# A half-swap of a 256 MB matrix by DMA alone: the sixteen engines on neighbouring rows instead of rows four apart

## The chip, the core and the metric

The kernel runs on one core of a Trainium2 chip. It uses none of the compute engines: all data is moved by the core's 16 DMA engines, straight from the input tensor in device memory (HBM) to the output tensor in the same memory. Two of the core's sequencers, SP (SyncE) and ACT (ScalarE), do nothing but issue DMA instructions and wait for older ones to land. Each of the two has a queue of its own, and both queues are served by the same 16 DMA engines.

The metric is the device time of one execution in microseconds (us). Beside it there is one profiled execution, whose trace records every DMA instruction, every DMA packet with its start and duration, and every semaphore wait.

## The reference

```
def setup_inputs():
    return {
        "x": np.random.randn(8192, 8192).astype(np.float32),
    }

def reference(x: np.ndarray) -> np.ndarray:
    return np.fft.ifftshift(x)
```

For an even number of rows and columns this shifts both axes by half: output row r is input row (r + 4096) mod 8192, and in each row the left and the right half change places. A row has 8192 float32 values, 32 KB; a half row, 16 KB, is the longest piece that stays in one piece. The matrix is 268.44 MB; all of it is read once and written once.

## The kernel before

The rows of the output are written in eight blocks of 1024 rows. Each block is written by eight DMAs, four on each queue. A DMA on SP's queue writes the left halves of 256 rows (reading the right halves of the source rows), and the DMA on ACT's queue that goes with it writes the right halves of the same rows (reading the left ones). So there are 32 DMAs on each queue, 64 in all, of 256 half rows, 4 MB, each.

Which 256 rows a DMA takes is in its access pattern, the list `dims` (line 30), which has three dimensions, each with a step in elements and a count:

- the outermost, `[STEP * C, ENGINES]`: 16 rows that lie STEP = 4 rows apart. This is the dimension over which a DMA is shared out to the 16 engines, one index for each.
- the middle one, `[STEP * ENGINES * C, per]`: each engine's own sequence of `per` = 16 rows, 64 rows apart.
- the innermost, `[1, hc]`: half a row, 4096 elements.

So at one moment the sixteen engines are to stand on sixteen rows that are 4 rows (128 KB) apart and cover 64 rows (2 MB), and each moves on by 64 rows. The loop on line 31 runs over the four rows `base` to `base + 3`: the first DMA of a block takes rows 0, 4, 8, ... of it, the next 1, 5, 9, ..., and after four the block is full. The pattern on the source side is the same, 4096 rows further on (modulo 8192).

There is no planner's order beyond this. The framework gives the DMAs eight semaphores in turn, so that each queue has four of its DMAs under way; before it issues the fifth, the sequencer waits until the first has landed. These waits carry the line of the DMA, L34; the waits at the end of the program carry L65, the line on which the tile context is left.

Of the kernel before, what the change touches and what calls it, by code (L numbers as in the profile page):

```python
# [1 line left out]

# [4 lines left out]


ENGINES = 16
STEP = 4  # L10


@with_exitstack
def kernel(
    ctx: ExitStack,
    tc: tile.TileContext,
    x: bass.AP,
    out: bass.AP,
):
    nc = tc.nc  # L20
    R, C = x.shape
    hr = R // 2
    hc = C // 2


    blocks = [(1024, 16)] * 8
    base = 0
    for rows, per in blocks:
        assert rows == STEP * ENGINES * per
        dims = [[STEP * C, ENGINES], [STEP * ENGINES * C, per], [1, hc]]  # L30
        for row in range(base, base + STEP):
            src_row = (row + hr) % R
            for eng, h in ((nc.sync, 0), (nc.scalar, hc)):
                eng.dma_start(  # L34
                    out=bass.AP(out.tensor, out.offset + row * C + h, dims),
                    in_=bass.AP(x.tensor, x.offset + src_row * C + hc - h, dims),
                )
        base += rows
    assert base == R


# [1 line left out]
_INS = ['x']  # L43
_OUTS = [((8192, 8192), 'float32')]


def kernel(**inputs):
    import numpy as _np
    import concourse.bacc as _bacc
    import concourse.tile as _tile  # L50
    from concourse import mybir as _mybir
    from concourse.bass_utils import run_bass_kernel_spmd as _run

    nc = _bacc.Bacc("TRN2", target_bir_lowering=False, num_devices=1)  # L54
    arrays, args = {}, []
    for name in _INS:
        a = _np.ascontiguousarray(inputs[name])
        if a.dtype.kind in "iu":
            a = a.astype(_np.int64)
        arrays[f"in_{name}_dram"] = a  # L60
        args.append(nc.dram_tensor(f"in_{name}_dram", a.shape, _mybir.dt.from_np(a.dtype), kind="ExternalInput").ap())
    for i, (shape, dtype) in enumerate(_OUTS):
        dt = _mybir.dt.from_np(_np.dtype(dtype))
        args.append(nc.dram_tensor(f"out_{i}_dram", shape, dt, kind="ExternalOutput").ap())
    with _tile.TileContext(nc) as tc:  # L65
        kernel(tc, *args)
    r = _run(nc, [arrays], core_ids=[0])
    got = tuple(r.results[0][f"out_{i}_dram"] for i in range(len(_OUTS)))
    return got[0]
```

## Time and profile before

| | |
|---|---|
| median of 3 runs | 824.26 us (824.24 to 824.76) |
| profiled execution, its span | 809.3 us |
| DMA instructions | 32 on SP, 32 on ACT, 4096 KB each |
| duration of a DMA instruction on its sequencer, median | 571 ns on SP, 578 ns on ACT |
| from issue to landing, shortest, median, longest | 25.1, 100.7, 103.1 us (both queues) |
| last DMA issued | at 705.9 us on SP, at 710.7 us on ACT |

The profiled execution's span runs from its first to its last recorded instruction; the device time of a run holds some work of the launch in addition. No other time than the span is known for the profiled execution.

A queue's share is the time that its packets took, as a part of what 16 engines have in the span. A packet here is one piece of up to 16 KB that one engine moves; packets under 512 bytes are the completions that an engine sends when its part of a DMA has landed. In a table of stretches the columns are: the stretch (us from the start of the span), its length, the busy time of the one compute engine that shows any work (GpSimd, four tiny instructions that set constants), the granted TensorE clock, the mean busy share of the 16 DMA engines (which can come out above 1 in short stretches, where a packet is counted whole), and the rate in GB/s, counted one way. In a list of waits the columns are who waited and on which line, for what, the total in us, the number of waits and the longest.

### The profile page before, as it was taken

Reading aid. Unit: us, or ns where it says so; the run is one execution under the profiler, and the core shown is the slowest. Engines: PE = TensorE matmul, PEld = TensorE weight load, DVE = VectorE, ACT = ScalarE, POOL = GpSimd, SP = SyncE. Lnnn points to the kernel's source line nnn. Section 1 sums busy time; section 2 is a strip of 40 time slices with the busy share of each in tenths; the row PEclk is TensorE's granted clock in tenths of the full one; section 3 lists DMA queues with packets and bytes.
Section 4 is the critical chain, followed back from the end, with each engine's and each line's share of the span. In section 5 each row is a group of like instructions: output and inputs, shape, how many; then the busy total and the mean of one; then the engine's idle time right before and its main releaser. Section 6 shows DMA issues by size and latency. Waiting matters only on the chain. (4 is left out here: it accounts for less than half of the span.)

```text
span 809.3 us, 109 instructions
## 1 busy us (share of the span) xinstructions
POOL 0.2 (0%) x4
## 2 busy tenths in 40 slices
POOL 0000000000000000000000000000000000000000
DMA  9999999999999999999999999999999999999998
GB/s 309 327 333 332 331 337 336 325 337 336 334 331 329 332 333 337 331 337 331 334 331 332 334 330 336 334 335 330 334 332 331 337 332 337 333 339 329 334 336 300
DMA packets 17408, 268.44 MB, mean 332 GB/s; under 512 B 1024, under 2 KB 1024, under 8 KB 1024
## 3 DMA queue, kind: packets, MB, share of 16 engines
q10 hardware_dynamic: 8704, 134.22, 49.9%
q1 hardware_dynamic: 8704, 134.22, 49.5%
HBM read 268.44 MB, written 268.44 MB: 663 GB/s over the span
## 5 line engine op out<-in xcount | busy, mean ns | idle before, releaser
L54 POOL MEMSET const-bfloat16-1.0<- 128x1 bf16 x1 | 0.1, 101 | 0.0
L54 POOL MEMSET const-uint8-127<- 128x1 uint8 x1 | 0.1, 101 | 0.0
L54 POOL MEMSET const-float32-0.0<- 128x1 f32 x1 | 0.1, 98 | 0.2 <-issue 0.2
L54 POOL MEMSET const-float32-1.0<- 128x1 f32 x1 | 0.1, 98 | 0.0
## 6 DMA issues: line engine op xcount, KB each, us to landing
out_dram<-in_x_dram ACTq DMA_DIRECT2D x32, 4096.0 KB, 100.7
out_dram<-in_x_dram SPq DMA_DIRECT2D x32, 4096.0 KB, 100.6
```

The lines of the kernel that those rows point to most:

```text
L54: nc = _bacc.Bacc("TRN2", target_bir_lowering=False, num_devices=1)
```

## The change

The constant STEP and the blocks go. A DMA now takes 512 neighbouring rows: its outermost dimension is 16 rows that lie one row (32 KB) apart, its middle one 32 steps of 16 rows (512 KB). There are 16 DMAs of 8 MB on each queue, 32 in all. The halves, the queues that they go to, and the order of the row ranges from the top down stay as they were.

```diff
-STEP = 4
...
-    blocks = [(1024, 16)] * 8
-    base = 0
-    for rows, per in blocks:
-        assert rows == STEP * ENGINES * per
-        dims = [[STEP * C, ENGINES], [STEP * ENGINES * C, per], [1, hc]]
-        for row in range(base, base + STEP):
-            src_row = (row + hr) % R
-            for eng, h in ((nc.sync, 0), (nc.scalar, hc)):
-                eng.dma_start(
-                    out=bass.AP(out.tensor, out.offset + row * C + h, dims),
-                    in_=bass.AP(x.tensor, x.offset + src_row * C + hc - h, dims),
-                )
-        base += rows
-    assert base == R
+    per = 32
+    dims = [[C, ENGINES], [ENGINES * C, per], [1, hc]]
+    for row in range(0, R, ENGINES * per):
+        src_row = (row + hr) % R
+        for queue, h in ((nc.sync, 0), (nc.scalar, hc)):
+            queue.dma_start(
+                out=bass.AP(out.tensor, out.offset + row * C + h, dims),
+                in_=bass.AP(x.tensor, x.offset + src_row * C + hc - h, dims),
+            )
```

## The prediction, made before the changed kernel was run

> **What bounds the kernel now.** I read the head of the page and its queue part first, because the kernel has no compute: the span, the number of packets, and how much of the sixteen DMA engines' time they fill.
>
> ```profile
> span 809.3 us, 109 instructions
> ...
> DMA packets 17408, 268.44 MB, mean 332 GB/s; under 512 B 1024, under 2 KB 1024, under 8 KB 1024
> ## 3 DMA queue, kind: packets, MB, share of 16 engines
> q10 hardware_dynamic: 8704, 134.22, 49.9%
> q1 hardware_dynamic: 8704, 134.22, 49.5%
> HBM read 268.44 MB, written 268.44 MB: 663 GB/s over the span
> ```
>
> The two queues fill 49.9 + 49.5 = 99.4% of the engines' time. Of 17408 packets, 1024 are tiny (64 DMAs with one completion on each of 16 engines), which leaves 16384 packets of 268.44 MB / 16384 = 16 KB: half a row each, 1024 per engine. One takes 0.994 x 809.3 us x 16 / 16384 = 0.786 us, and 1024 of them one after another make 804.6 us. So the end is set by what a 16 KB packet takes, and by nothing else.
>
> Second, stretches of the span, for what lies around the packets.
>
> ```profile
> core 0: us, POOL busy (x), PEclk, DMA share, GB/s
> 0.00:2.10 2.10, 0.20 (x4) 1.00 0.00 0
> 2.10:8.00 5.90, 0.00 (x0) 1.00 1.00 355
> 8.00:14.00 6.00, 0.00 (x0) 1.00 1.01 344
> ...
> 101.00:401.00 300.00, 0.00 (x0) 1.00 1.00 333
> ...
> 808.00:809.30 1.30, 0.00 (x0) 1.00 0.00 0
> ```
>
> Ahead of the first packet lie 2.1 us, behind the last 1.3: 3.4 us without data. The other 805.9 us move it at 333 GB/s, evenly from 100 us on, but faster (355, 344) in the first 12 us. The median of the runs, 824.26 us, is 15.0 us above the profiled span; I keep these 15.0 us unchanged, so a time is data + 3.4 + 15.0 = data + 18.4.
>
> Third, the waits of the issuing queue, to see whether a late DMA ever starves the engines.
>
> ```profile
> SPq L34 <- DMA out_dram<-in_x_dram: 686.6, 28, 25.0
> SPq L65 <- DMA out_dram<-in_x_dram: 101.9, 2, 79.4
> ...
> out_dram<-in_x_dram SPq DMA_DIRECT2D x32, 4096.0 KB, 100.6
> ```
>
> SP issues 32 DMAs and waits before 28 of them, at most 25.0 us; four are always under way, and one lands 100.6 us after its issue (four times 25.2 us). While it waits, three DMAs, some 75 us of work, lie ahead of the engines. Nothing is starved.
>
> Fourth, stretches cut by data: the span cut wherever another 1/512 of all bytes has moved, which is one row of 32 KB for every engine. Eight of them, from the middle:
>
> ```profile
> 510.81:512.28 1.47, 0.00 (x0) 1.00 1.10 368
> 512.28:513.96 1.68, 0.00 (x0) 1.00 0.84 283
> 513.96:515.48 1.52, 0.00 (x0) 1.00 1.10 356
> 515.48:517.16 1.68, 0.00 (x0) 1.00 0.94 312
> 517.16:518.64 1.48, 0.00 (x0) 1.00 1.10 365
> 518.64:520.24 1.60, 0.00 (x0) 1.00 0.93 317
> 520.24:521.77 1.53, 0.00 (x0) 1.00 1.10 353
> 521.77:523.46 1.69, 0.00 (x0) 1.00 0.91 301
> ```
>
> The second column is the time of one row step (the rate, in so short a stretch, depends on which packets' starts fall into it). Four steps take 1.47, 1.52, 1.48, 1.53, mean 1.50 us; the four between them 1.68, 1.68, 1.60, 1.69, mean 1.66. The work is the same, the engines are full in both; what differs is which rows the sixteen stand on and how they stand to each other. So a packet's price is not a constant of an engine, it depends by about 10% on the set of addresses under way at once. That is the quantity that this change touches. I also followed each engine through the trace (its next packet starts 3 to 4 ns before its last one ends): the sixteen alternate strictly between the queues, and their packet counts lie within 2 of each other at 50 us and within 6 at 600 us. They move almost in step, so "which addresses at once" is well described by the pattern.
>
> **The change, part by part.**
>
> *Bytes and packets.* The last dimension stays half a row, so there are again 16384 packets of 16 KB, 1024 an engine, one from the left and one from the right half in turn. Nothing is saved there: 0.
>
> *Half as many DMAs.* 32 instead of 64, 8 MB instead of 4. Each queue issues 16 fewer at 0.57 to 0.58 us (the issue rows' medians, 571 ns on SP and 578 on ACT): 9.2 us less on each of two queues that spend 686.6 us waiting. Hidden by the waits: 0. If four DMAs weren't queued ahead, the same 9.2 us would stand on the path; they are, and with 8 MB each, four of them cover about 200 us instead of 100. What is queued behind an issuing instruction is only the next issue.
>
> *Half as many completions.* 32 fewer tiny packets per engine. The rest of the data time beyond packets, 805.9 - 804.6 = 1.3 us, is all that 64 completions and the seams between DMAs can cost, so 32 of them cost 0 to 0.7 us. I take -0.3.
>
> *Start and end.* The first packet comes 1.4 us after the first issue at 0.73 us. An instruction with twice the rows could take up to twice that before its first packet: 0 to +1.4; the sixteen first packets start within 1 us of each other although each stands for 16 rows, so I take 0. At the end the last DMA of each queue is larger but an engine's share of the whole is not; the engines' packet counts differ by up to 6, which would cost up to 6 x 0.786 = 4.7 us if it all fell on the last engine, and the tail here costs about 1 us. -1 to +3.7, taken 0.
>
> *Where the engines stand.* Before, neighbouring engines were 4 rows (128 KB) apart, the sixteen covered 64 rows (2 MB), and the next step was 2 MB on; the rows between were filled by the next three DMAs. After, neighbours are 1 row (32 KB) apart, the sixteen read one closed piece of 512 KB and write one of 512 KB, and the next step is 512 KB on. The trace has no row for this distance. The bounds are the two kinds of row step: all 512 steps at 1.50 us make 768.0 us, time 786.4; all at 1.66 make 849.9, time 868.3. Today's mean, 805.9 / 512 = 1.574, is half of each. I take three slow to two fast: (3 x 1.66 + 2 x 1.50) / 5 = 1.596 us, x 512 = 817.2. Why on the slow side: today's fast steps alternate with slow ones, so whatever makes a step fast lasts for one step of 2 MB and depends on how the engines' addresses differ; the change makes them differ less, by a quarter of the distance both between engines and from step to step, and packs reads and writes alike into a quarter of the address range. With less difference between the addresses under way, I expect more of the unfavourable meetings than of the favourable ones. This is the weak term; the trace shows that placement matters, not which way.
>
> The Trainium skill ("DMA: Bandwidth & Descriptors", Latency and other measured facts) has a rule that speaks against my sign: copies between HBM tensors lost rate when rows lay a large power of two apart, 207 GB/s per direction at 512 KiB and 164 at 2 MiB. If it held for an engine's step, 2 MB before and 512 KB after, the data time would be 805.9 x 164 / 207 = 638 us and the time 657, an estimate from that page; if it held for the distance between neighbouring engines, both kernels would be on its good side and nothing would change. The row is 333 GB/s per direction at a step of 2 MB, above both of the page's figures, so I give the rule no weight in the sum.
>
> **Sum.** 817.2 (row steps) - 0.3 (completions) + 3.4 (around the data) = 820.3 us of span, + 15.0 = 835.3; I say 836 for the open ends of the start and the tail.
>
> **The rivals.**
>
> *The closed piece is served better (faster).* For it: placement is worth 10%, and the first 12 us, when all engines start level, run at 355 and 344 GB/s rather than 333; if neighbouring rows keep that opening rate (mean 350), 268.44 MB / 350 GB/s = 767 us, and half of that gain gives (805.9 + 767) / 2 = 786.5 us, time 804.9. Against it: the opening is also the time in which queues are still filling, and it lies at the old distance.
>
> *The rate belongs to the traffic, not to the place (no change).* For it: every long stretch gives 333 to 335 GB/s although the engines drift. Then only the small terms are left: 824.26 - 0.3 = 824.0, within 1% either way. Against it: the row steps above. The same time results if the change doesn't do what it says, because the engines drift: a few rows of drift are now as long as the distance between neighbours, and the pattern blurs.
>
> *All engines meet at one place (much slower).* Sixteen engines that stand at the same offset in neighbouring rows could get in each other's way at every step. Price: the longest of the row steps that I cut in this stretch, 529.52 to 531.31, 1.79 us; x 512 = 916 us, time 935. It decides as soon as the steps no longer alternate. Against it: at 4 rows' distance the opening steps show nothing of it.
>
> The Trainium skill ("HBM Reference", Specifications) gives about 716 GB/s for the memory of a pair of cores; 536.9 MB at that would be 750 us, time 768, an estimate, which would leave the faster rival room and no more; the row is 663 GB/s over the span.
>
> **How the numbers follow.** Moderately slower 0.45, much slower 0.08, faster 0.32, unchanged 0.15. What can be told from no change here is about 0.2%, 1.6 us; the unchanged case spreads by 1%, and gives 0.06 within that, 0.05 slower and 0.04 faster. So slower 0.45 + 0.08 + 0.05 = 0.58, faster 0.32 + 0.04 = 0.36, same 0.06. The likeliest case alone reaches from 826 to 868. The range goes from 786, all steps fast, to 878, all steps slow and 10 us for the way to the much slower case and the start and tail; some 0.06 lies below and 0.09 above.
>
> **What would show it.** Completions: 512 tiny packets instead of 1024. Depth: 100.6 us to landing should become about 204, with 12 waits on SP of about 51 us. The weak term: the packet, from the queues' shares, should rise from 0.786 to about 0.797 us, and more than half of the row steps should be long. If the packet falls, the sign is wrong, and the first rival holds; if it stays within 0.008 us, the second. If the queues' share falls well below 99%, the engines idle, and my statement that nothing starves is wrong.

## The result: 0.28% faster in the first comparison, and no change on another chip

The changed kernel took 821.94 us (median of 6 runs, 820.05 to 823.13), beside it the kernel before 824.38 us (823.05 to 824.86): a ratio of 0.9972, 95% interval 0.9962 to 0.9982. (A ratio here is worked out from all runs and can differ by up to 0.1% from the quotient of two medians.) The time is near the value that the second rival gave (824.0, within 1%). The forecast was 836, slower than before; the kernel became slightly faster.

This is the page of the changed kernel, its head and queue part:

```profile
span 821.2 us, 77 instructions
...
DMA packets 16896, 268.44 MB, mean 327 GB/s; under 512 B 512, under 2 KB 512, under 8 KB 512
## 3 DMA queue, kind: packets, MB, share of 16 engines
q1 hardware_dynamic: 8448, 134.22, 50.2%
q10 hardware_dynamic: 8448, 134.22, 49.0%
HBM read 268.44 MB, written 268.44 MB: 654 GB/s over the span
...
out_dram<-in_x_dram SPq DMA_DIRECT2D x16, 8192.0 KB, 204.0
```

The page shows half as many completions (512), the doubled time to landing (204.0 us), and a packet of 0.992 x 821.2 us x 16 / 16384 = 0.796 us. Set beside the 0.786 us of the page before, this looks like a kernel that became slower by 1.2%, and the span rose from 809.3 to 821.2 us, while the median fell. Two pages that contradict two medians are the first thing to clear up. The profiled execution of the changed kernel took 822.98 us, 1.8 us above its span, and so it is in every execution for which both are known (1.7 to 2.1 us). So the kernel before, profiled at 809.3 us, took about 811 us in that execution, not 824: the two profiles come from chips of different speed, as the next section shows, and no work of 15 us lies outside the span.

The stretches of the changed kernel (stretch, length, busy GpSimd, clock, share of the DMA engines, GB/s) show the same shape as before, at a lower level, and a longer end:

```profile
0.00:2.10 2.10, 0.20 (x4) 1.00 0.00 0
2.10:8.00 5.90, 0.00 (x0) 1.00 1.01 353
8.00:14.00 6.00, 0.00 (x0) 1.00 1.03 333
101.00:401.00 300.00, 0.00 (x0) 1.00 1.00 329
...
815.00:817.00 2.00, 0.00 (x0) 1.00 1.06 369
817.00:819.00 2.00, 0.00 (x0) 1.00 0.33 123
819.00:821.20 2.20, 0.00 (x0) 1.00 0.02 7
```

The start is unchanged (first packet after 2.1 us), and the opening rate of 353 has dropped to 333 in the second stretch. In the last 4 us the engines run out one after another.

### The profile page after: what moved, and what is told of

The parts are those of the page before. It is cut to its first block, busy times and chain, and to the rows that moved or that the text cites. A ratio compares the mean times of both kernels' runs of the same rounds, so it can differ in the third digit from the quotient of the medians.

```text
span 821.2 us, 77 instructions
## 1 busy us (share of the span) xinstructions
POOL 0.2 (0%) x4
## 6 DMA issues: line engine op xcount, KB each, us to landing
out_dram<-in_x_dram SPq DMA_DIRECT2D x16, 8192.0 KB, 204.0
```

## The experiments

The kernels ran in five groups, each group on one chip, beside the kernel before on the same chip ("this call" in the expectations is such a group). That kernel took 810.8, 824.0, 811.8, 811.1 and 810.8 us in them: three different chips of one kind (811 us; the last two groups ran on the same chip) and one of another (824 us), to which the first comparison seems to belong. I write "811 kind" and "824 kind"; the second stands for this one chip. Every ratio is to the kernel before on the same chip.

The theories to be told apart: **the place** (neighbouring rows are served better), **the size** (half as many DMAs save seams), **the traffic** (memory serves a fixed total as long as no arrangement is bad, and the 0.28% is a detail of the chip). The prediction's own step, that a closer placement costs, stood as the fourth.

### The kernel before against itself

No edit.

> The kernel before, unchanged, timed against itself and profiled on this chip. It prices what a comparison of this kind can tell, and says whether the profiled span of 809.3 us belongs to the kernel. If the 15.0 us between the span shown and the median are work of the launch outside the span, its span is again about 809 and its packets take 0.786 us. If they are a different chip or a different moment, its span is about 822 us and its packets take about 0.797 us. Both expect a ratio of 1.000 within 0.002.

> The kernel before, for a trace of it on the same chip as the changed kernel's. If both kinds of chip serve the same packets at different speed and nothing else differs, its time is span + 1.8 us, and the packet is 0.786 us where the time is 811 us and about 0.798 us where it is 824.

> The kernel before, for its trace on this call's chip. Where it takes 824 us the packet should be about 0.798 us, against 0.795 for the changed kernel there, and the row steps should alternate as on the other kind (correlation of neighbouring steps about -0.6). Where it takes 811 us, as before: 0.785 us.

Measured: 811.05 beside 810.79 us, ratio 1.0003 (0.9995 to 1.0012); the single runs 811.08 and 810.88 us; spans 808.4, 809.3 and 809.1. All three fell to the 811 kind. The queue lines of the first:

```profile
span 808.4 us, 109 instructions
...
q10 hardware_dynamic: 8704, 134.22, 50.0%
q1 hardware_dynamic: 8704, 134.22, 49.4%
```

0.994 x 808.4 x 16 / 16384 = 0.785 us a packet: the profile before was of this kind of chip. The span of about 809 us, which the first expectation ties to 15 us of launch work, came here with a time of 810.17 us in the same execution, so it speaks for the other explanation, a different chip. No trace of the kernel before fell to the 824 kind.

### The place alone, the size alone

```diff
 place:  -STEP = 4            +STEP = 1
         -blocks = [(1024, 16)] * 8   +blocks = [(256, 16)] * 32
 size:   -blocks = [(1024, 16)] * 8   +blocks = [(2048, 32)] * 4
```

> Only the placement: engines on neighbouring rows, but DMAs of 4 MB, 64 of them, as before. If the placement makes the gain, the ratio is about 0.997, as for the whole change. If the half as many DMAs make it, the ratio is 1.000.

> Only the size: engines four rows apart as before, but 32 DMAs of 8 MB. If the half as many DMAs make the gain (completions and seams, worth 0 to 0.7 us by the prediction, 2.4 us if they are all of it), the ratio is 0.997. If the placement makes it, 1.000 to 0.9992.

> The placement alone, beside the whole change in the same call. If the placement alone makes whatever difference there is, its ratio agrees with that of the whole change within 0.002; if the size adds something, the whole change is lower by up to 0.001 (0.7 us of completions).

> The size alone again. On the 811 us kind it gave 1.0005. If completions and seams cost at most the 0.7 us of the prediction, 0.999 to 1.001 on either kind; if the size makes a part of the gain on the 824 us kind, 0.998 to 0.999 there.

> The size alone. On the 811 us kind it gave 1.0005 and 0.9999, and does so again if this call falls on one. On the 824 us kind: 1.000 if the gain there is all of the placement, 0.9985 if the half as many DMAs bring about half of it (the placement alone gave 0.9988 there, the whole change 0.9972 and 0.9977).

> The size alone, once more. On the 811 us kind it has given 1.0005, 0.9999 and 1.0000. If this call falls on the 824 us kind: 1.000 and packets of about 0.798 us if the gain there is all of the placement; 0.9985 and packets of 0.797 if half of it comes with the half as many DMAs.

Measured:

```
place alone, 811 kind   812.46 us   1.0022 (1.0010 to 1.0034)
place alone, 824 kind   822.43 us   0.9988 (0.9975 to 1.0001)
size alone, 811 kind    811.22 us   1.0005 (0.9996 to 1.0013)
size alone, 811 kind    811.76 us   0.9999 (0.9990 to 1.0008)
size alone, 811 kind    811.21 us   1.0000 (0.9992 to 1.0009)
size alone, 811 kind    811.05 us   1.0005 (0.9996 to 1.0014)
```

The size does nothing on the 811 kind, four times over; it never met the 824 kind. The place alone is 0.2% slower on the one kind. On the other its interval reaches from no change (1.0001) to the gain of the whole change (0.9975), so there the place and the size can't be told apart. What the 811 kind shows is that the gain doesn't belong to the placement as such.

### The whole change again

> The changed kernel once more, beside the kernel before, on whatever chip this falls to (the time of the kernel before tells which kind: 811 or 824 us). If the gain of the first comparison belongs to the kernel, the ratio is 0.997 on either. If it belongs to the chip, it is 0.997 where the kernel before takes 824 us and 1.002 where it takes 811, as the placement alone gave there.

> The changed kernel beside the kernel before for the third time. Where the kernel before takes 824 us, the ratio is 0.997 to 0.998, as twice already. Where it takes 811 us: if the placement's gain belongs to the chip, 1.000 to 1.003, as the placement alone gave there; if the gain belongs to the whole change on every chip, 0.997.

Measured: on the 824 kind 821.69 us, 0.9977 (0.9963 to 0.9990); on the 811 kind 813.04 us, 1.0005 (0.9993 to 1.0017). The quotient of the two medians is 1.0015 on the 811 kind (813.04 / 811.84). So the first comparison is confirmed on the 824 kind, and the one chip of the 811 kind that ran the whole change shows no gain: the intervals don't overlap. The queue lines on the 811 kind:

```profile
span 811.4 us, 77 instructions
...
q1 hardware_dynamic: 8448, 134.22, 49.9%
q10 hardware_dynamic: 8448, 134.22, 49.3%
```

0.992 x 811.4 x 16 / 16384 = 0.786 us a packet, where the kernel before has 0.785 on that kind: the same packet, to a thousandth. The 0.796 us of the first page was the chip.

### How far apart may the engines be?

Four kernels with 4 MB a DMA. In the first three each engine goes down `own` = 16, 64 or 256 rows of its own, one by one; in the last it jumps.

```diff
...
+    dims = [[own * C, ENGINES], [C, per], [1, hc]]
...
-STEP = 4
+STEP = 16
-    blocks = [(1024, 16)] * 8
+    blocks = [(4096, 16)] * 2
```

> DMAs of 4 MB; each engine goes down 16 rows of its own one by one, neighbouring engines are 16 rows (512 KB) apart. If near distances are all alike and only a far one costs, 0.99 to 1.02. If the cost grows steadily from 32 KB to the 8 MB that took 2.09 times as long, about 1.3 (half of the way in doublings: 4 of 8 beyond 32 KB).

> As the one before with 64 rows (2 MB) between neighbouring engines. Near distances alike up to here: 0.99 to 1.02. A steady growth: about 1.7 (6 of 8 doublings). A loss that is already whole at 2 MB: 2.0.

> DMAs of 4 MB as before, but each engine on 256 rows of its own in each half of the matrix, so that neighbouring engines are 256 rows (8 MB) apart and each moves on by one row. If the rate belongs to the traffic, not to the place, the ratio stays within 0.99 to 1.01. If the prediction's step was right that the place decides, and only its sign at short distances was wrong, it is clearly off: 1.04 (all row steps at 1.66 us) or more, or 0.95 (all at 1.50).

> The kernel before with STEP = 16 and 4 MB as before: neighbouring engines are 16 rows (512 KB) apart, and each moves on by 256 rows (8 MB) at a time. If only the distance between engines costs, and not how far one engine jumps, 0.995 to 1.01, as with 512 KB and steps of one row (0.9972). If a jump of 8 MB costs as a distance of 8 MB does, near 2.

Measured, with the distance between neighbouring engines and the step of one engine:

```
512 KB, step 32 KB   824 kind    821.09 us   0.9972 (0.9958 to 0.9985)
2 MB,   step 32 KB   824 kind   1354.80 us   1.60 to 1.66 (four runs of 1322 to 1370)
8 MB,   step 32 KB   811 kind   1697.17 us   2.0946 (2.0919 to 2.0973)
512 KB, step 8 MB    811 kind    857.57 us   1.0582 (1.0565 to 1.0599)
```

The pages of the 8 MB distance and of the 8 MB step, one line each of their shares and totals:

```profile
q10 hardware_dynamic: 8704, 134.22, 49.3%
...
HBM read 268.44 MB, written 268.44 MB: 317 GB/s over the span
```

```profile
q10 hardware_dynamic: 8704, 134.22, 49.7%
...
HBM read 268.44 MB, written 268.44 MB: 628 GB/s over the span
```

The engines are as full as ever (49.3 and 49.7% for one of two queues); a packet only takes longer, 1.63 us in the first. So the place can cost a factor of two, but of the distances tried only 2 MB and 8 MB cost anything: from 32 KB over 128 to 512 KB the ratio stays within 0.3%. A steady growth from 32 KB on is out. The expectation put it at 1.3 for 512 KB (the reckoning that gave 1.7 for 2 MB would give 1.45); neither came. All these distances are powers of two and no run has one that isn't, so whether the distance costs or the power of two isn't shown. The jump of one engine matters too, much less: 5.8% at 8 MB. I had expected up to 1% or a factor near 2 there, and both were wrong. The Trainium skill ("DMA: Bandwidth & Descriptors", Latency and other measured facts) has copies at 207 GB/s per direction with rows 512 KiB apart, at 164 with 2 MiB and at 103 with 4 and 8 MiB, and at 214 again, which it calls full, with 4 MiB padded by 4 KiB. Its distances are between rows and those here between engines; the runs agree in kind, with 0.997, 1.60 to 1.66 and 2.09 in time for engines 512 KB, 2 MB and 8 MB apart. No run here shows the padding. For this change, with 128 KB before and 32 KB after, the row decides nothing.

### Two regions at once

Neighbouring rows, 4 MB; SP's queue does the top half of the matrix and ACT's the bottom half, both halves of a row in turn.

```diff
+    for row in range(0, hr, ENGINES * per):
+        for h in (0, hc):
+            for queue, top in ((nc.sync, 0), (nc.scalar, hr)):
+                src_row = row + hr - top
...
```

> Neighbouring rows and 4 MB as in the placement alone, but the two queues work on the top and the bottom half of the matrix, so that at every moment two regions 128 MB apart are read and two written. If the total of reads and writes sets the rate wherever it is near enough, 0.99 to 1.01. If the meeting of addresses matters at this level too, off by more than 0.02, as with 2 MB between engines (1.64).

Measured (811 kind): 813.72 us, 1.0023 (1.0007 to 1.0040), a packet of 0.784 us. Reads and writes in two regions 128 MB apart cost what one region costs, to 0.4%: being far apart is not in itself dear. The kernel behaves as the place alone does on this kind, 1.0022.

### Reading alone, writing alone

```diff
 reading:
...
+            t = pool.tile([128, hc], mybir.dt.float32)
+            queue.dma_start(out=t[:], in_=x[row:row + 128, h:h + hc])
 writing:
...
+            queue.dma_start(out=out[row:row + 128, h:h + hc], in_=t[:])
```

> All of the matrix is read once into on-chip memory, in the same 16 KB pieces by the same two queues, and only one piece of the output is written; the rest of the copy is left out. If the engines set the 0.786 us of a packet, it stays at about 0.78 us and the time near 800 us. If memory that is read and written at once sets it, the packet falls to the 0.61 us that the quickest packets of the copy take, and the time to about 1024 x 0.61 + 5 = 630 us.

> One 2 MB piece is read once and written to all of the output from on-chip memory; the rest of the reading is left out, so the output is not the shifted matrix. Reading alone ran at the 0.61 us a packet. If it is only both at once that takes 0.786, writing alone is also near 0.61 us and 640 us in all. If writing is the slow side, it stays near 0.78 us and 810.

Measured (811 kind, one run each): 639.29 us and 641.87 us. Here a DMA has 2 MB, and its other end is on-chip memory. The lines of the page for reading, then for writing:

```profile
DMA packets 18578, 270.56 MB, mean 424 GB/s; under 512 B 2064, under 2 KB 2064, under 8 KB 2064
## 3 DMA queue, kind: packets, MB, share of 16 engines
q1 hardware_dynamic: 9360, 136.32, 50.4%
q10 hardware_dynamic: 9216, 134.22, 49.4%
```

```profile
DMA packets 18576, 270.54 MB, mean 423 GB/s; under 512 B 2064, under 2 KB 2064, under 8 KB 2064
## 3 DMA queue, kind: packets, MB, share of 16 engines
q1 hardware_dynamic: 9360, 136.32, 50.2%
q10 hardware_dynamic: 9216, 134.22, 49.6%
```

In the first, 18578 - 2064 = 16514 packets are left; two of them fetch instructions, and 16512 have 16 KB. The engines are full, 0.998 of 637.5 us: 0.998 x 637.5 x 16 / 16512 = 0.616 us each when reading, and 0.998 x 639.8 x 16 / 16512 = 0.619 us when writing. The copy takes 0.785.

Is 0.785 us then what one engine needs to read and write at once? The packets of the copies say no. In the trace of the kernel before, 29% of them take 0.608 to 0.615 us. And at the end, when engines run out one after another, the price falls: in the last 6 us of the fifteen traces with engines 32 to 512 KB apart (all but those with 2 MB, 8 MB and the 8 MB step), 57 packets ran while on average at most eight engines were busy, and 51 of them took 0.608 to 0.615 us. They read and wrote device memory like all others. So the mean is set neither by an engine nor by one direction, but by something that the sixteen share when all of them copy.

At 0.611 us a packet, sixteen engines would read 429 GB/s and write as much, 858 in all; the copy gets 664. Reading alone, 428 GB/s in its long stretches, and writing alone run at that price of an engine, so these two runs don't show what the memory could give in one direction. That the total of 663 to 664 GB/s is the memory's own limit, and not one of the way to it, is the likeliest account, but not shown. It is what both kernels have in common.

## Why the prediction was wrong

**Bytes, packets and the engines as the bound**: right. The queues fill 99.2% of the engines' time after the change as 99.4% before, nothing starves, and 16384 packets remain.

**Half as many DMAs**: right in the price, 0, and wrong in the account. Completions fell to 512, the landing time is 204.0 us as forecast, and the size alone is worth nothing that can be told (1.0005, 0.9999, 1.0000, 1.0005). But the prediction counted an issue of 8 MB at the 0.57 us of one of 4 MB, and twelve waits of about 51 us each. The waits of the changed kernel (total us, number, longest):

```profile
SPq L30 <- DMA out_dram<-in_x_dram: 134.4, 12, 51.3
```

Only the longest has 51 us; the twelve make 134.4 us in all. In place of waiting, the sequencer stands in the issuing instruction itself: on SP it takes a median of 41.3 us, where the kernel before has 571 ns, and 40.9 us in the first run of the size alone. Why, no run shows. It cost nothing, because the queues still filled 99.2% of the engines' time.

**The 15.0 us around the span**: wrong. The span and the median came from chips of different speed; span and time of one execution differ by 1.8 us. The sum starts at the right level, 824, only because the 15 us stood for the slower chip. They should have been doubted, since nothing in the page gave a cause for them.

**Where the engines stand**: this step failed, in its premise. The prediction took the long and short row steps for two prices, 1.66 and 1.50 us, that belong to how the engines stand, and re-weighted them three to two, for 1.596 us a step. The same cut of the changed kernel's trace (again one row of 32 KB for every engine in each line; 811 kind):

```profile
514.37:515.94 1.57, 0.00 (x0) 1.00 1.14 355
515.94:517.67 1.73, 0.00 (x0) 1.00 0.84 284
517.67:519.13 1.46, 0.00 (x0) 1.00 1.00 381
519.13:520.59 1.46, 0.00 (x0) 1.00 1.18 382
520.59:522.31 1.72, 0.00 (x0) 1.00 0.83 267
522.31:523.90 1.59, 0.00 (x0) 1.00 1.06 350
523.90:525.40 1.50, 0.00 (x0) 1.00 0.87 328
525.40:526.97 1.57, 0.00 (x0) 1.00 1.14 355
```

The second column doesn't alternate strictly, short steps follow short ones, and still the mean of the eight is 12.60 / 8 = 1.575 us. Nor was the strict alternation typical of the kernel before: the eight lines of the prediction were a clear stretch. The same cut of another of its traces (811 kind) has little of it:

```profile
513.69:515.28 1.59, 0.00 (x0) 1.00 1.00 330
515.28:516.87 1.59, 0.00 (x0) 1.00 0.97 330
516.87:518.39 1.52, 0.00 (x0) 1.00 1.04 345
518.39:519.98 1.59, 0.00 (x0) 1.00 1.00 330
519.98:521.58 1.60, 0.00 (x0) 1.00 1.01 338
521.58:523.11 1.53, 0.00 (x0) 1.00 1.04 353
523.11:524.74 1.63, 0.00 (x0) 1.00 0.86 281
524.74:526.32 1.58, 0.00 (x0) 1.00 1.07 353
```

Over the whole of each trace (480 steps each, worked out from the packets' starts and durations):

```
                               kind  packet ns   step us  neighbouring steps  engine idle us
before (4 traces)              811   784 to 785   1.57     -0.61 to -0.66      1.2 to 1.9
size alone (4)                 811   784 to 786   1.57     -0.56 to -0.65      1.0 to 2.1
place, top/bottom, change (3)  811   784 to 786   1.57     -0.31 to -0.35      2.5 to 3.6
change (2), place, 512 KB      824   795       1.59 to 1.60  -0.21 to -0.29      2.8 to 3.6
step of 8 MB                   811   830          1.66     -0.41               -
```

"Neighbouring steps" is the correlation of a step's time with the next one's. "Kind" is that of the chip; "engine idle" is what one engine stands idle, on average, between the first packet and the end of the last one. On the 811 kind, engines four rows apart alternate more strongly (-0.6) than engines on neighbouring rows (-0.3), and the step's mean is the same to 0.005 us. (How strongly depends on the cut: with steps cut at the ends of packets it is -0.55 to -0.62 against -0.44 to -0.54.) A step that is long is made up for by later ones. In the trace of the kernel before, single steps scatter by 0.10 us (standard deviation), and sums of 32 steps by 0.17 us, where steps independent of each other would give 0.57; in that of the changed kernel it is 0.09, 0.18 and 0.51. So the alternation is how a nearly fixed total is spread over time, not a choice between two prices. The share of steps above 1.58 us, half way between the two prices, is 48% in the changed kernel and 43 to 49% in the four traces of the kernel before, not "more than half". Changing the pattern changed the alternation and left the total alone. The term was sized at 817.2 - 805.9 = +11.3 us. On the 811 kind the whole change measures +0.4 us by the ratio of 1.0005 (+1.2 us by the medians), with an interval from -0.6 to +1.4; on the 824 kind -2.3 us in the first comparison. Some 3 of the 11.3 us came from the eight lines alone: their two means make 1.58 us on average, where the whole trace has 1.574.

The prediction's test, a packet that rises from 0.786 to about 0.797 us, came out at 0.796 and would have confirmed the wrong step, because it compared traces of two chips. On one kind of chip it fails: 0.785 and 0.786.

**The rivals.** The second, that the rate belongs to the traffic and not to the place, had it right for distances up to 512 KB; as a general rule the run with 8 MB refutes it (2.09 where it expected 0.99 to 1.01). The fast first 12 us were no evidence for the first: neighbouring rows have the same fast opening (353 beside 355 GB/s) and lose it as well. The third, a much slower kernel, did not come at neighbouring rows; a place can cost that much, but at 2 MB and 8 MB.

**What is left of the 0.28%.** On the 811 kind the packets are equal, and the last column shows what little remains: an engine on neighbouring rows idles 2.5 to 3.6 us, one four rows apart 1.0 to 2.1. Here are the last stretches of the place alone, where it measured 1.0022:

```profile
803.00:805.00 2.00, 0.00 (x0) 1.00 1.01 311
805.00:807.00 2.00, 0.00 (x0) 1.00 0.71 246
807.00:810.10 3.10, 0.00 (x0) 1.00 0.09 37
```

And those of the kernel before on the same chip:

```profile
802.00:804.00 2.00, 0.00 (x0) 1.00 0.90 279
804.00:806.00 2.00, 0.00 (x0) 1.00 1.23 418
806.00:808.40 2.40, 0.00 (x0) 1.00 0.08 27
```

The engines of the place alone run out over some 4 us (0.71, then 0.09), those of the kernel before within about 2 (1.23, then 0.08); an uneven end of 1 to 2 us is the size of the 1.7 us between 812.46 and 810.79. The prediction had taken 0 for the tail, from a range of -1 to +3.7. On the 824 kind the end is as long, so the gain should be in the packets, and exceed what the longer end takes: if the kernel before has 1.5 us of idling there too, its packet would be (824.0 - 1.8 - 3.4 - 1.5) / 1024 = 0.798 us, against the 0.795 measured for the changed one. That is an estimate; no trace of the kernel before on that kind exists to show it. The kernel with engines 512 KB apart, with 4 MB and 64 DMAs as before, has the same 0.9972 there, so the halved number of DMAs isn't needed for a gain of this size, and neighbouring rows aren't either. Why that chip serves all this 1.6% slower (the chip itself, or something else that used its memory at the time), and four rows' distance 0.2 to 0.3% slower still, stays open.

## What to carry to other kernels

When DMA engines are full and the copy goes from device memory to device memory, look first at what all engines together reach (here 663 to 664 GB/s of reads and writes, while a packet beside few others takes 0.611 us in place of 0.785), and price a new arrangement by that total. Short swings in a trace that make up for each other are no prices: take sums of many steps, from more than one stretch and one trace, before you call one. Don't spend work on the order of engines that stand 32 to 512 KB apart; keep them from standing 2 MB or 8 MB apart, where this copy took 1.6 and 2.1 times as long. Compare a profile only with a profile of the same chip, and a span with the time of its own execution: 1.6% between chips buried an effect of 0.3%, and the gain of 0.3% on one chip was none on the other that ran both kernels.

## What the hardware did that I had not expected

Chips differ: the same kernel takes 811 us on three and 824 on another, and the changed kernel fills 99.2% of the engines' time on both kinds, with packets of 0.786 and 0.795 us. A loss appears somewhere between 512 KB and 2 MB of distance between engines (0.997, 1.60 to 1.66, and 2.09 at 8 MB). An engine that jumps by 8 MB at each row costs 5.8%, though its fifteen companions stay as near as in a kernel that loses nothing. And issuing a DMA of 8 MB held SP's sequencer for a median of 41.3 us, one of 4 MB for 0.57. The Trainium skill ("HBM Reference", Specifications) gives a core streaming alone about 425 GB/s and calls that bounded by its 16 DMA engines; reading alone here agrees, with 424 and engines 99.8% full.
